# Triangular products of two heads: one PSUM bank per class of product, masked into two tiles

## The chip, the cores and the metric

The kernel runs on one core of one Trainium2 chip. The metric is the device time of one execution in microseconds (us); smaller is better. A core has five engines that run side by side, each through its own list of instructions in a fixed order: TensorE (PE: matmuls out of SBUF into PSUM, with weight loads that the profile lists apart as PEld), VectorE (DVE), ScalarE (ACT), GpSimd (POOL) and SyncE (SP, which here only issues DMAs). They wait for each other through semaphores. PSUM, into which TensorE writes, has eight banks of 512 float32 per partition, on 128 partitions.

## The reference, cut to what matters

The reference is one inference step of two layers, on a prompt of 512 tokens and on eight short sample sequences. Layer 0 is an RWKV-7 time mixing, layer 1 a sparse attention. The change touches only the recurrence of layer 0 for the prompt. There are 16 heads of width 64, and each holds a 64 x 64 state S that every token updates:

```python
def step(S, inp):
    r_t, w_t, k_t, v_t, a_t, b_t = inp
    sa = jnp.einsum('bhij,bhj->bhi', S, a_t)
    S = S * w_t[:, :, None, :] + sa[..., None] * b_t[:, :, None, :] + v_t[..., None] * k_t[:, :, None, :]
    return S, jnp.einsum('bhij,bhj->bhi', S, r_t)
```

The kernel doesn't take the 512 tokens one by one. It takes eight chunks of 64 tokens, and inside a chunk it works with matrices "token by token" (64 x 64). Such a matrix says how much the key of token s adds to the answer of token t. A token sees only earlier ones, so these matrices are triangular: the full product is computed, and a mask (`gmask`) sets the other half to zero.

## The kernel before, in words

`layer0` first projects the inputs, then computes keys, decays and rates (`keys`), inverts small triangular systems (`invert`, `merge`), and then runs the recurrence from about 331 us to 545 us of the profiled span. After that come the output projection of layer 0 (`project_out`, whose matmuls stand under the helper line 326) and layer 1 (`layer1`).

**Heads, pairs and groups.** The 16 heads lie in eight pairs. One head of a pair is on partitions 0 to 63, the other on partitions 64 to 127; `PARS` lists the two halves as `(r, par)`. Four pairs make a group g (0 or 1). The function `chunk(c, g, ...)` handles one chunk c of one group, so it runs 8 x 2 = 16 times. It is a generator. Lines 867 to 911 drive it: the stages that need no state (up to the masks) run for the next chunk while the current chunk goes through the stages that do, group 1 lags two chunks behind group 0, and after each step some "filler" is drawn: the gates, the sample recurrence, the output projection of the first half, all with matmuls of their own.

**One call of `chunk`.**
- Lines 1128 to 1131 load AR (per head the vectors a and r, scaled by the decay, 64 + 64 columns) and BK (per head keys k and b) from DRAM, by SP's queue, into tiles `ab0`/`ab1`.
- For an even chunk, lines 1135 to 1143 transpose the values into `sav`; lines 1146 to 1150 transpose BK into `bt`.
- Lines 1153 to 1159 are the triangular products. There are two classes. **Own** (line 1156): one factor of a head (k for one half of the partitions, b for the other, see line 1025) against both of its columns a and r, 64 x 128 outputs, which land on the head's own partitions. **Other** (line 1159): the other factor against r alone, 64 x 64 outputs, which land on the other half of the partitions. Each class has eight matmuls in a call. Before, there is one bank for each head of the pairs: `pg[0]` takes own and other of the heads with par 0, `pg[1]` those of par 1. The two banks come from the tag `pr`, which has two buffers in all; `pr` also serves the transposes of lines 1135 and 1146 and the output `py` of line 1201, for both groups.
- Lines 1160 to 1165 multiply the products with the mask and write them to two SBUF tiles `G[0]`, `G[1]` of 4 x 128 floats per partition (tag `q0`/`q1`): two instructions of 64 partitions (line 1162, the columns of a) and two of 128 partitions (line 1164, the columns of r), 256 elements per partition each.
- Lines 1169 to 1178 compute `s0` from G's columns of a and from the state; lines 1180 to 1185 apply the inverse; lines 1187 to 1199 make the new state; lines 1201 to 1211 make the output `py` from the state and from G's columns of r.

**What sets the order.** The program text gives priorities only. The whole kernel is built in a `TileContext` with `schedule_with_timeline_sim=True` (line 2119): a planner goes through the instructions with its own model of their times, gives each tile a buffer of its tag when one comes free, and writes down a fixed list for each engine. A matmul whose PSUM tile has no buffer yet is passed over for other work that has. Reads and writes of one PSUM bank by different engines are kept apart bank by bank: a mask of a bank waits for the last matmul into that bank.

Of the kernel before, what the change touches and what calls it, by code (L numbers as in the profile page):

```python
# [13 lines left out]
OP = mybir.AluOpType  # L14
# [207 lines left out]
PARS = [(slice(0, 64), 0), (slice(64, 128), 1)]  # L222


class K:
# [898 lines left out]
    def chunk(self, c, g, NTt, VT, PC, dAR, dBK, STS, Y):  # L1124
        nc = self.nc
        ident, gmask = self.C("ident"), self.C("gmask")
        ps = range(4 * g, 4 * g + 4)
        AR = self.t(f"ab{g}", (128, 4, 2, 64))
        nc.sync.dma_start(AR.rearrange("p i x n -> p i (x n)"), dAR[g][:, :, c])
        BK = self.t(f"ab{g}", (128, 4, 2, 64))  # L1130
        nc.sync.dma_start(BK.rearrange("p i x n -> p (i x) n"), dBK[g][:, :, :, c].rearrange("p i x n -> p (i x) n"))
        if c % 2 == 0:

            tk = c * 64 + (16 if c >= 4 else 0)
            pv = self.t("pr", (128, 4, 2, 64))
            for i, p in enumerate(ps):
                nc.tensor.transpose(pv[:, i].rearrange("p a b -> p (a b)"), VT[p][:, tk:tk + 128], ident)
            for x in range(2):
                r = slice(x * 64, x * 64 + 64)
                sav = self.t(f"q{g}", (128, 4, 2, 64))  # L1140
                for par in range(2):
                    nc.scalar.activation(sav[par * 64:par * 64 + 64, :, par, :], pv[r, :, par, :], AF.Copy)
                self.SA[g, c + x] = sav
        sav = self.SA[g, c]
        yield
        pb = self.t("pr", (128, 4, 128))
        for i in range(4):
            nc.tensor.transpose(pb[:, i], BK[:, i].rearrange("p a b -> p (a b)"), ident)
        bt = self.t(f"q{g}", (128, 4, 128))
        nc.scalar.activation(bt, pb, AF.Copy)  # L1150
        yield

        pg = [self.t("pr", (128, 4, 128)) for _ in range(2)]
        for i in range(4):
            for r, par in PARS:
                nc.tensor.matmul(pg[par][r, i], BK[r, i, par], AR[r, i].rearrange("p a b -> p (a b)"), start=True, stop=True)  # L1156
        for i in range(4):
            for r, par in PARS:
                nc.tensor.matmul(pg[par][PARS[1 - par][0], i, 64:128], BK[r, i, 1 - par], AR[r, i, 1], start=True, stop=True)
        G = [self.t(f"q{g}", (128, 4, 128)) for _ in range(2)]  # L1160
        for r, par in PARS:
            nc.vector.tensor_tensor(G[par][r, :, 0:64], pg[par][r, :, 0:64], gmask[r, None, 0:64].to_broadcast([64, 4, 64]), OP.mult)
        for r, par in PARS:
            nc.vector.tensor_tensor(G[par][:, :, 64:128], pg[par][:, :, 64:128],
                                    gmask[:, None, 64:128].to_broadcast([128, 4, 64]), OP.mult)
        yield
        ST = STS[g]

        s0 = self.t(f"s{g}", (128, 4, 64))
        for i in range(4):  # L1170
            for r, par in PARS:
                nc.tensor.matmul(s0[r, i], G[par][r, i, 0:64], sav[r, i, par], start=(i == 0), stop=(c == 0), skip_group_check=True)
        if c > 0:
            for i in range(4):
                for r, par in PARS:
                    nc.tensor.matmul(s0[r, i], AR[r, i, 0, :], ST[r, i], start=False, stop=True, skip_group_check=True)
        s0s = self.t(f"f{g}", (128, 4, 64))
        nc.vector.tensor_copy(s0s, s0)
        yield
        sa = self.t(f"s{g}", (128, 4, 64))  # L1180
        for i, p in enumerate(ps):
            for r, par in PARS:
                nc.tensor.matmul(sa[PARS[1 - par][0], i], NTt[p][r, c], s0s[r, i], start=True, stop=True)
        nc.vector.tensor_copy(sav[64:128, :, 0, :], sa[64:128])
        nc.vector.tensor_copy(sav[0:64, :, 1, :], sa[0:64])
        yield
        pS = self.t(f"s{g}", (128, 4, 64))
        for i in range(4):
            for r, par in PARS:
                nc.tensor.matmul(pS[r, i], bt[:, i, r], sav[:, i, par], start=True, stop=True)  # L1190
        st = self.t(f"f{g}", (128, 4, 64))
        pc = PC[:, 4 * g:4 * g + 4, c:c + 1].to_broadcast([128, 4, 64])
        if c > 0:
            tt = self.t(f"f{g}", (128, 4, 64))
            nc.vector.tensor_tensor(tt, pS, ST, OP.add)
            nc.vector.tensor_tensor(st, tt, pc, OP.mult)
        else:
            nc.vector.tensor_tensor(st, pS, pc, OP.mult)
        STS[g] = st
        yield  # L1200
        py = self.t("pr", (128, 4, 64))
        if c > 0:
            for i in range(4):
                for r, par in PARS:
                    nc.tensor.matmul(py[r, i], ST[r, i], AR[r, i, 1, :], start=(i == 0), stop=False, skip_group_check=True)
        for i in range(4):
            for r, par in PARS:
                nc.tensor.matmul(py[r, i], sav[:, i, par], G[par][:, i, 64:128], start=(c == 0 and i == 0), stop=True, skip_group_check=True)
        if c % 2 == 0:
            Y[g].append(self.t("p", (128, 2, 4, 64)))  # L1210
        nc.scalar.activation(Y[g][-1][:, c % 2], py, AF.Copy)
        yield
# [910 lines left out]
```

## Time and profile before

| what | value |
|---|---|
| time before, median of 3 runs | 1035.68 us (1035.01 to 1036.47) |
| the profiled execution | 1032.77 us, of which its span is 1031.0 us |
| PE busy (matmuls) | 949.3 us, 92% of the span |
| DVE busy | 666.8 us, 65% |
| ACT busy | 565.8 us, 55% |
| POOL busy | 474.3 us, 46% |
| DMA | 156.69 MB, mean 152 GB/s |

The span is what the profile sees of one execution, from the first to the last instruction; 1.77 us of the execution lie around it. The profiled execution was 2.91 us (0.28%) faster than the median of the other runs. An engine is busy when one of its instructions runs; matmuls overlap each other, so a busy PE says that something was in it, and the time that a set of matmuls takes is read from the start of the first to the start of what follows. A float32 matmul stands in the trace as two records: line 1156 issues 16 x 8 = 128 matmuls and has 256 records. The chain of work follows the last instruction back to what released it, step by step, and so tells which engine was the late one in each stretch.

### The profile page before, as it was taken

What the parts mean: (1) busy time and instruction counts of PE and PEld (TensorE: products, weight loads), DVE (VectorE), ACT (ScalarE), POOL (GpSimd) and SP (SyncE); (2) the same over time, 40 slices, a digit from 0 to 9 for tenths busy, and PEclk for the clock granted to TensorE, in tenths of its full rate; (3) what the DMA queues carried; (4) which work ended last, traced back from release to release, by engine and by line L of the source; (5) the groups of instructions that cost most, each with busy time, mean ns of one, the idle gap of its engine ahead of it and who ended that gap; (6) DMA issues with size and microseconds to landing.
All of it is one profiled execution on the core that took longest, in us unless ns stands there. A gap on an engine that the chain in (4) does not pass through costs nothing.

```text
span 1031.0 us, 24779 instructions
## 1 busy us (share of the span) xinstructions
PE 949.3 (92%) x9429; PEld 845.1 (82%) x9429; DVE 666.8 (65%) x1504; ACT 565.8 (55%) x1333; POOL 474.3 (46%) x573
## 2 busy tenths in 40 slices
PE   5799998989989999999898989999999999987997
PEld 4798997979777868888787988999788887875986
DVE  3797579798486642556966824655785566477554
ACT  4356685556444336435544635656686657475442
POOL 5923558654930363221323475665353547233530
PEclk8798999999999999999998999999999999998999
DMA  5675525648645454655594642332444462454533
GB/s 186 198 258 192 186 68 158 191 132 241 208 134 143 135 169 146 185 149 131 123 274 126 209 142 84 115 109 84 119 125 129 106 164 82 145 166 151 176 122 113
DMA packets 151368, 156.69 MB, mean 152 GB/s; under 512 B 53330, under 2 KB 99954, under 8 KB 150994
## 3 DMA queue, kind: packets, MB, share of 16 engines
q1 hardware_dynamic: 151250, 155.11, 50.6%
q8 instruction: 74, 1.21, 0.5%
q14 instruction: 44, 0.36, 0.1%
HBM read 111.33 MB, written 43.93 MB: 151 GB/s over the span
## 4 chain that ended last, share of the span: by engine, by line
PE 46%; DVE 11%; DMA 6%; POOL 4%; ACT 4%; issue 3%; SPq 1%; DVEq 0%; POOLq 0%; ACTq 0%
PE ph L326 21%; PE pq L1726 3%; PE pw L1820 3%; PE pq L1804 2%; POOL l L288 2%; PE pr L1156 2%; DMA d<-dram 2%; PE ph L2046 1%; ACT a L1760 1%; DVE a L1780 1%; DVE l L288 1%; ACT l L287 1%; PE ph L371 1%; DMA out_swkv<-p 1%; DVE a L1753 1%
## 5 line engine op out<-in xcount | busy, mean ns | idle before, releaser
L326 PE MATMUL ph<-x,l 128*128 128x272 f32 x2448 | 362.6, 299 | 13.4 <-ACT x L287 4.0
L326 PEld LDWEIGHTS ph<-x,l 128*128 128x128 f32 x2448 | 327.7, 193 | 31.5 <-issue 7.3
L288 POOL TENSOR_TENSOR l<-w,l 128x512 fp32r<-128x512 f32 (+2 forms) x118 | 157.7, 1349 | 139.3 <-ACT l L287 120.5
L287 ACT ACTIVATE l<-w 128x512 fp32r<-128x512 f32 (+2 forms) x160 | 93.6, 612 | 100.1 <-PE ph L326 43.6
L326 PE MATMUL pp<-x,l 128*128 128x272 f32 x768 | 111.5, 300 | 6.0 <-POOL l L288 6.0
L326 PEld LDWEIGHTS pp<-x,l 128*128 128x128 f32 x768 | 103.9, 195 | 8.4 <-POOL l L288 6.2
L1760 ACT ACTIVATE a<-a,st 128x512 f32<-128x512 f32 (+3 forms) x128 | 70.7, 554 | 26.5 <-DVE st L1753 25.9
L1753 DVE CUSTOM_DVE_ANT_0 a<-pq,tb 128x512 f32<-128x512 f32 (+3 forms) x128 | 56.7, 484 | 21.3 <-PE pq L1726 21.0
L1726 PE MATMUL pq<-p,z 128*128 128x512 f32 (+7 forms) x288 | 57.0, 326 | 3.1 <-DVE st L1756 1.5
L326 PE MATMUL pp<-t,l 128*128 128x272 f32 x384 | 54.9, 294 | 0.0
L1807 ACT ACTIVATE h<-pq 128x512 f32<-128x512 f32 x60 | 35.4, 591 | 34.0 <-PE pq L1804 27.3
L1804 PE MATMUL pq<-cst,a 128*128 128x128 f32 x320 | 49.5, 278 | 3.7 <-DVE st L1756 1.8
L326 PEld LDWEIGHTS pp<-t,l 128*128 128x128 f32 x384 | 50.8, 190 | 0.9
L1780 DVE TENSOR_SCALAR a<-a,st 128x128 f32<-128x128 f32 (+3 forms) x112 | 50.9, 514 | 0.5
L288 POOL TENSOR_TENSOR d<-d,d 128x544 fp32r<-128x544 f32 (+2 forms) x21 | 28.8, 1370 | 48.4 <-ACT d L287 38.9
L1726 PEld LDWEIGHTS pq<-p,z 128*128 128x128 f32 x288 | 42.3, 189 | 9.7 <-issue 5.0
L288 DVE TENSOR_TENSOR l<-w,l 128x512 fp32r<-128x512 f32 x42 | 35.7, 860 | 15.5 <-ACT l L287 15.3
L1804 PEld LDWEIGHTS pq<-cst,a 128*128 128x128 f32 x320 | 37.0, 141 | 9.9 <-issue 7.6
L1500 DVE TENSOR_TENSOR d<-ph,RS 128x272 f32<-128x272 f32 x56 | 24.1, 436 | 31.1 <-PE ph L326 29.9
L1820 PE MATMUL pw<-h,p 128*64 128x256 f32 x320 | 38.8, 390 | 1.1 <-ACT h L1807 0.7
L1773 POOL TENSOR_TENSOR cc<-cc,st 128x64 f32<-128x64 f32 x32 | 12.6, 395 | 52.7 <-DVE st L1770 43.5
L667 POOL TENSOR_TENSOR d<-d,d 128x544 f32<-128x544 f32 x8 | 11.2, 1397 | 55.7 <-ACT d L385 55.7
(419 smaller groups left out, 2011.1 us busy)
## 6 DMA issues: line engine op xcount, KB each, us to landing
w<-in_rkvz SPq DMA_DIRECT2D x64, 256.0 KB, 2.9
d<-dram SPq DMA_DIRECT2D x54, 272.0 KB, 4.2
w<-in_win SPq DMA_DIRECT2D x56, 256.0 KB, 2.9
dram<-d SPq DMA_DIRECT2D x48, 272.0 KB, 2.6
ab<-dram SPq DMA_DIRECT2D x32, 256.0 KB, 3.6
p<-in_xT SPq DMA_DIRECT2D x16, 272.0 KB, 3.9
tb<-dram SPq DMA_DIRECT2D x16, 264.0 KB, 5.2
dram<-uar SPq DMA_DIRECT2D x8, 512.0 KB, 3.5
```

The source lines that it names most:

```text
L287: nc.scalar.activation(hi, raw, AF.Copy)
L288: (eng or nc.gpsimd).tensor_tensor(lo, raw, hi.bitcast(F32), OP.subtract)
L326: nc.tensor.matmul((pt[h][:m, :HN] if split else pt[:m, h, :HN]), a[:, k, :m], b[:, h * HN:(h + 1) * HN], start=(k == 0 and n == 0), stop= ...
L1156: nc.tensor.matmul(pg[par][r, i], BK[r, i, par], AR[r, i].rearrange("p a b -> p (a b)"), start=True, stop=True)
L1500: self.nc.vector.tensor_tensor(o, p, r, OP.mult)
L1726: nc.tensor.matmul(p[:, par], QZ[k, b][x][:, par, m], kk[:, lo:hi], start=(x == 0), stop=(x == 1))
L1753: nc.vector.tensor_tensor_reduce(out=P[par][j], in0=p[:, par, :n], in1=TB[k][:, g, o:o + n], scale=-1.0, scalar=3.0e38, op0=OP.add, op1=OP ...
L1760: nc.scalar.activation(P[par][j], P[par][j], AF.Exp, scale=-1.0, bias=st[:, 0, g, j + 1:j + 2], accum_out=st[:, 1, g, j + 1:j + 2])
L1780: (nc.gpsimd if e == "p" else nc.vector).tensor_scalar(pj, pj, rr, None, op0=OP.mult)
L1804: nc.tensor.transpose(pt[:, g % 2, g // 2], PB[g][j][:, c * 128:c * 128 + 128], ident)
L1807: nc.scalar.activation(w, pt, AF.Copy)
L1820: nc.tensor.matmul(po[r], v, W[x][:, par], start=False, stop=(x == 0), skip_group_check=True)
```

## The change

The two banks of the products are divided by class and no longer by head. `own` takes the own products of both heads of the pairs (each head on its own partitions, 128 columns per pair); `other` takes the other products of both (64 columns per pair). The masks write two tiles: `GA` for the columns of a of both heads in one instruction of 128 partitions, and `GR` for the columns of r, in four instructions of 64 partitions each. Every mask instruction has 256 elements per partition, as before; there are five where there were four. The readers take the same numbers from the new tiles: `s0` (line 1172) from `GA`, `py` (line 1208) from `GR`. The number and the shapes of the matmuls are the same, and so is the number of tiles taken from `pr` and from `q0`/`q1`.

```diff
-        pg = [self.t("pr", (128, 4, 128)) for _ in range(2)]
+        own, other = self.t("pr", (128, 4, 128)), self.t("pr", (128, 4, 64))
         for i in range(4):
             for r, par in PARS:
-                nc.tensor.matmul(pg[par][r, i], BK[r, i, par], AR[r, i].rearrange("p a b -> p (a b)"), start=True, stop=True)
+                nc.tensor.matmul(own[r, i], BK[r, i, par], AR[r, i].rearrange("p a b -> p (a b)"), start=True, stop=True)
         for i in range(4):
             for r, par in PARS:
-                nc.tensor.matmul(pg[par][PARS[1 - par][0], i, 64:128], BK[r, i, 1 - par], AR[r, i, 1], start=True, stop=True)
-        G = [self.t(f"q{g}", (128, 4, 128)) for _ in range(2)]
+                nc.tensor.matmul(other[PARS[1 - par][0], i], BK[r, i, 1 - par], AR[r, i, 1], start=True, stop=True)
+        GA, GR = self.t(f"q{g}", (128, 4, 64)), self.t(f"q{g}", (128, 2, 4, 64))
+
+        def masked(r, x):
+            return gmask[r, None, x * 64:x * 64 + 64].to_broadcast([r.stop - r.start, 4, 64])
+
+        nc.vector.tensor_tensor(GA, own[:, :, 0:64], masked(slice(0, 128), 0), OP.mult)
         for r, par in PARS:
-            nc.vector.tensor_tensor(G[par][r, :, 0:64], pg[par][r, :, 0:64], gmask[r, None, 0:64].to_broadcast([64, 4, 64]), OP.mult)
+            nc.vector.tensor_tensor(GR[r, par], own[r, :, 64:128], masked(r, 1), OP.mult)
         for r, par in PARS:
-            nc.vector.tensor_tensor(G[par][:, :, 64:128], pg[par][:, :, 64:128],
-                                    gmask[:, None, 64:128].to_broadcast([128, 4, 64]), OP.mult)
+            nc.vector.tensor_tensor(GR[r, 1 - par], other[r], masked(r, 1), OP.mult)
...
-                nc.tensor.matmul(s0[r, i], G[par][r, i, 0:64], sav[r, i, par], start=(i == 0), stop=(c == 0), skip_group_check=True)
+                nc.tensor.matmul(s0[r, i], GA[r, i], sav[r, i, par], start=(i == 0), stop=(c == 0), skip_group_check=True)
...
-                nc.tensor.matmul(py[r, i], sav[:, i, par], G[par][:, i, 64:128], start=(c == 0 and i == 0), stop=True, skip_group_check=True)
+                nc.tensor.matmul(py[r, i], sav[:, i, par], GR[:, par, i], start=(c == 0 and i == 0), stop=True, skip_group_check=True)
```

## The prediction, made before the changed kernel ran

> **What bounds the kernel now.** I read the page first, then busy times by stretch for the recurrence, then the chain of work through it.
>
> ```profile
> span 1031.0 us, 24779 instructions
> PE 949.3 (92%) x9429; PEld 845.1 (82%) x9429; DVE 666.8 (65%) x1504; ACT 565.8 (55%) x1333; POOL 474.3 (46%) x573
> ```
>
> PE is the fullest engine, but that is a mean over stages. The products run only in the recurrence, so I cut that into four stretches (columns: start and end, length, then busy us and instructions of PE, PEld, DVE, ACT, POOL; granted TensorE clock, DMA share, GB/s).
>
> ```profile
> 331.00:395.00 64.00, 60.41 (x836) 48.74 (x836) 33.37 (x65) 24.08 (x49) 27.63 (x27) 0.97 0.50 144
> 395.00:488.00 93.00, 92.81 (x1621) 80.80 (x1622) 47.33 (x112) 45.83 (x107) 26.47 (x22) 1.00 0.54 159
> 488.00:511.00 23.00, 19.51 (x341) 16.17 (x341) 20.43 (x71) 12.76 (x42) 9.33 (x16) 1.00 0.47 111
> 511.00:545.00 34.00, 32.13 (x429) 28.05 (x425) 23.53 (x59) 15.87 (x35) 8.16 (x9) 1.00 0.88 236
> ```
>
> From 395 to 488 PE is busy 92.81 of 93.00 us and DVE only 47.33. From 488 to 511 it turns round: DVE 20.43 of 23.00. From 511 the DMAs are full (0.88). The chain of work (start, us, what) says the same, with the edges between the stretches:
>
> ```profile
> by line: PE pr L1156 13.3%; PE ph L326 11.6%; PE ph L371 8.6%; PE s L1172 5.3%; PE pr L1148 5.0%; PE s L1183 4.8%; PE s L1190 4.6%; PE pr L1208 4.2%; DVE p L733 4.0%; PE s L1176 3.7%; PE pr L1159 3.6%; PE pr L1205 3.3%; PE ph L720 2.7%; DMA
> 386.00 3.48 DMA q<-dram
> 395.18 0.68 PE s L1109 x32
> 491.99 0.43 DVE q L1162
> 508.20 0.79 DVE p L733 x3
> ```
>
> The first row is the share by line of the chain from 395 to 511 us: the own products (L1156) alone are 13.3% of it, more than any other line, and the other products (L1159) 3.6%. Until 386 the chain came through a DMA (and before that through POOL), so PE time saved earlier than 395 moves nothing. From 395.18 it lies on PE; at 491.99 it goes over to DVE.
>
> What follows the recurrence hangs on its end. SP, the DMA queue (waits: total us, times, longest):
>
> ```profile
> SPq L914 <- DVE f L1195: 7.1, 1, 7.1
> 511.74 0.35 SPq L914 DMA_DIRECT2D out_pwkv<-f  x1
> ```
>
> SP stood 7.1 us before line 914, which stores the last state of group 0; the loads behind it make the full DMAs from 511 on. If that state comes earlier, they come earlier. So I take a gain on the chain before 511 to reach the end whole.
>
> **The products on PE, the term that decides.** Timeline and chain rows of PE, four ways in which products and their like run today:
>
> ```profile
> 437.01 0.76 PE L1156 MATMUL pr<-ab,ab 64*64 64x128 f32 x5
> 437.50 0.27 PE L1159 MATMUL pr<-ab,ab 64*64 64x64 f32 x1
> 437.61 0.27 PE L1156 MATMUL pr<-ab,ab 64*64 64x128 f32 x1
> ...
> 438.11 0.39 PE L371 MATMUL ph<-p,p 128*128 128x272 f32 x1
> ...
> 438.88 0.69 PE pr L1156 x5
> 439.97 0.95 PE ph L371 x6
> ...
> 338.99 0.71 PE L1156 MATMUL pr<-ab,ab 64*64 64x128 f32 x10
> 340.06 0.29 PE L1312 MATMUL ph<-p,v 32*32 32x64 f32 x2
> ...
> 461.25 0.65 PE L1156 MATMUL pr<-ab,ab 64*64 64x128 f32 x8
> 461.83 1.02 PE L326 MATMUL ph<-x,l 128*128 128x272 f32 x6
> ...
> 432.89 0.61 PE s L1183 x16
> 433.50 0.70 PE ph L371 x4
> ```
>
> First, a bank alone. Between 437.01 and 438.11 stand eight records of L1156 and eight of L1159, that is four own and four other matmuls (two records each): the products of the heads of one par, one bank. Then PE does something else (L371), and the second bank follows at 438.88, until 439.97. The heads of one par all use the same 64 x 64 part of PE, so the own records start one by one, 0.11 us apart (437.50 to 437.61). A bank costs 1.10 us (438.11 - 437.01), the second 1.09; a call 2.2 us.
>
> Second, both banks at once. At 338.99 the two banks were both free, the planner alternates the two halves, and the records start in pairs: the whole call takes 340.06 - 338.99 = 1.07 us.
>
> Third, 461.25: half of the own products of both heads, alternating (eight records one by one would take 0.9), 0.58 us until L326. The other four matmuls are four more pairs of records, 0.11 us each: a whole own class alone would take 0.58 + 0.44 = 1.02 us.
>
> Fourth, L1183: sixteen records of 64 columns, alternating between the two halves of the partitions, into **one** bank (the tile `s`): 0.61 us. That is the shape of the other class after the change.
>
> After the change a bank holds both halves, so each pass alternates even when the two banks come free at different times: 1.02 + 0.61 = 1.63 us for a call instead of 2.2, a gain of **0.57 us**. If the two passes stand together, it is 1.07, a gain of 1.13 us. A call that had both banks at once already gains nothing. I take 0.57, since the halves stand apart in nearly every call today, and the tag `pr` still has two buffers.
>
> ```profile
> 395.00:488.00 93.00, 18.87 (x147) 14.63 (x148) 1.00 0.54 159
> 488.00:511.00 23.00, 6.33 (x47) 4.69 (x45) 1.00 0.47 111
> ```
>
> These are the L1156 records (PE, then PEld) in two stretches: 147 / 16 = 9 calls between 395 and 488, 47 / 16 = 3 between 488 and 511. Of the nine, the one at 461.25 alternates already. PE term: 8 x 0.57 = **4.6 us**, at most 8 x 1.13 = 9.0, at least 0 (if other work that stands on PE between passes takes the place). The four calls outside 395 to 511 and the three in the DVE stretch I count at nothing on PE: there the chain lies on POOL, DMA and DVE; were PE late there, they would add 7 x 0.57 = 4.0.
>
> The Trainium skill speaks against this. Its page "TensorEngine Tiling (Array Packing)", section "Gotcha 1: PSUM Pressure", says that different row tiles can't access the same PSUM bank at the same time; after the change the two heads of a pair are two row tiles in one bank. The trace disagrees for writes to different partitions: L1183 has just this, and its sixteen records take 0.61 us; one by one, at half of 0.11 us each for 64 columns, they would take some 0.9. What the rule would give is a rival below.
>
> **The masks on DVE.** (Duration ns min/median/max, first and last start.)
>
> ```profile
> L1162 DVE TENSOR_TENSOR q<-pr,cst x32: 406/422/431, 332.8 to 524.9; 64x256 f32<-64x256 f32 x32
> L1164 DVE TENSOR_TENSOR q<-pr,cst x32: 402/415/427, 333.1 to 525.3; 128x256 f32<-128x256 f32 x32
> DVE q L1162 <- PE pr L1159: 22.5, 16, 9.8
> ```
>
> 64 partitions cost as much as 128 (422 and 415 ns), so what counts is the number: five instead of four in each of 16 calls, 16 x 0.42 = 6.7 us more of DVE. Between 395 and 488 it is hidden: DVE is busy 47.33 of 93.00 us, and the 9 x 0.42 = 3.8 us fit. Between 488 and 511 DVE is the chain: 3 x 0.42 = **1.3 us** on the path. The first calls hide behind POOL and DMA, the last behind the full DMAs. If the cover went everywhere, the price would be 6.7.
>
> The masks' waits: today the first mask of a bank waits for the last other product (22.5 us in 16 waits, idle time of an engine that isn't late there). Afterwards GA waits for the own class alone and GR's last two for the other class. No wait is added to the list; behind a waiting mask stand the recurrence's copies (L1178, L1184, L1185) and the state (L1195) of the other group, for which PE waits with L1183 and L1190, as today. `s0` needs GA only and could start sooner; the masks run one chunk ahead of it, so I count nothing. Where the first mask's stall goes, PE is late next, not DVE.
>
> **What costs nothing.** Loads of weights: the same number and shapes. `GR` is read in one run instead of with gaps, `GA` lies alone: no row shows a difference by that, so I take 0, with a few ns each way as bounds. Buffers: two `pr` and two `q` tiles as before; GA is free after `s0` instead of after `py`; a gain or nothing. DMAs: none moves in the text; SP's load of the next BK waits for the last other product, as today.
>
> **Sum.** -4.6 + 1.3 = **-3.3 us**. The profiled execution (1032.77 us, span 1031.0 and 1.77 around it) would become 1029.5. It lies 2.9 below the median of the runs, 1035.68; from that median the forecast is **1032.4 us** (-0.32%).
>
> **Rivals.**
>
> *The passes stand together.* One class ends and the other bank is free at once: -9.0 + 1.3 = -7.7, **1028.0 us**. Against it: only two buffers of `pr`, shared with L1135, L1148 and py; for it: 338.99.
>
> *No change.* The PE gain is taken up again: the DVE stretch holds its 20.43 us of work and begins only when its inputs (finish, gates, loads) are there, or the DMAs from 511 on (share 0.88) don't start earlier. 0 of 4.6 arrives, or no more than the masks take back: **1035.7 us**. For it: three engines are the bound in turn within 150 us.
>
> *The ring of PSUM buffers, the other side.* A bank of `pr` now comes free after three masks (own), the other after two, where it was two and two; 0.42 us more per call before the next transposes (L1148) or `py` (L1205) may start. With two buffers for both groups that decides from the point at which PE runs out of other work while both are held. All 16 calls on the path, 6.7, and the 1.3 of the DVE stretch, less the 4.6: +3.4, **1039.1 us**; with no PE gain +6.7, 1042.4. The planner writes other lists for every engine too, and one bad place is worth as much:
>
> ```profile
> SPq L1131 <- PE pr L1159: 16.9, 5, 6.1
> PEld pr L1205 <- ACT p L1211: 0.9, 2, 0.6
> ```
>
> SP already stood up to 6.1 us at the loads of BK behind the other products. Against the ring: PE waited only 0.9 us for `pr` buffers at L1205, because fillers stand in.
>
> *Row tiles take turns in a bank.* Own records one by one: 1.02 + 8 x 0.11 = 1.90; other, at twice 0.61, 1.2; a call 3.1 instead of 2.2: 8 x 0.9 = 7.2, and 1.3 of masks: +8.5, **1044.2 us**. L1183 speaks against it; only the 128-column form in one bank is unseen. This is the skill's rule named above.
>
> **How the numbers follow.** A measurement of this kernel can tell about 0.2% (2.1 us) from no change: below 1033.6 is faster, above 1037.8 slower. Chances: the forecast 0.45 (its own range 1029 to 1034), together 0.08, no change 0.22, ring or a bad list 0.20, turns 0.05. Of the forecast 0.03 falls within 0.2%. Faster 0.42 + 0.08 = 0.50; same 0.03 + 0.22 = 0.25; slower 0.20 + 0.05 = 0.25. The range goes from the PE bound with a little replanning, 1026, to 1041, between the ring's two prices; outside are the turns and the tails of two rivals.
>
> **What would show it.** Right: own records start in pairs in nearly every call, from own's first record to the next line about 1.0 us, other about 0.6; 80 masks instead of 64, at 0.42 us; PE still full between 395 and 488, that stretch some 4 us shorter; line 914 about 3 us earlier. Wrong: own records one by one; PE idle in that stretch before L1148 or L1205; the chain on DVE before 480; line 914 earlier and the end not.

## The result, and the profile after

The changed kernel takes 1041.3 us in the median (1039.23 to 1045.71, 5 runs); the kernel before took 1035.01 beside it (1029.92 to 1036.47, 5 runs). The ratio is 1.0059, 95% interval 1.003 to 1.0087: slower by 0.6%, where 1032.4 was predicted, and 0.3 us above the top of the range. The ratios and their intervals come from the runs in the chip's usual, fast state, by another estimate than the quotient of the two medians, and can differ from it by up to 0.3%. The profiled execution of the changed kernel took 1043.79 us, with a span of 1042.0; that of before took 1032.77.

From line 1160 on the changed text stands up to four lines lower: the masks are lines 1165 (GA), 1167 (own into GR) and 1169 (other into GR), `py` is 1209 and 1212, its copy 1215.

The products do what the change says. The chain of work of the changed kernel (start, us, what):

```profile
446.98 1.02 PE pr L1156 x16
...
448.82 0.61 PE pr L1159 x16
...
462.55 1.02 PE pr L1156 x16
...
464.86 0.61 PE pr L1159 x16
```

Own takes 1.02 us and other 0.61, the very numbers of the prediction; the first pair holds in spite of what the clock did just before, as shown below. The four stretches of the recurrence, which the prediction shows of before (start and end, length, busy us of PE, PEld, DVE, ACT, POOL, then clock, DMA share, GB/s):

```profile
331.00:395.00 64.00, 60.18 (x832) 48.60 (x832) 34.78 (x67) 24.74 (x50) 28.37 (x27) 0.97 0.48 141
395.00:488.00 93.00, 84.08 (x1527) 72.61 (x1524) 46.28 (x108) 43.28 (x102) 25.43 (x21) 0.94 0.51 149
488.00:511.00 23.00, 18.31 (x356) 14.76 (x354) 19.59 (x61) 10.77 (x30) 6.50 (x9) 0.94 0.52 123
511.00:545.00 34.00, 30.26 (x427) 25.50 (x424) 23.46 (x62) 15.42 (x40) 6.88 (x9) 0.89 0.70 192
```

The second stretch was full before (92.81 of 93.00). Now PE stands for 8.9 us of it, and the granted clock falls to 0.94. So a large part of the loss lies where the gain was expected. (Of the 8.9 us, 3.6 lie before 425 us; they were not followed.) In the third and fourth stretch the clock is lower too, 0.94 and 0.89 where it was 1.00; more on this under "Wait or clock?". Cut finer, around 431 us, the changed kernel shows:

```profile
422.00:431.00 9.00, 7.67 (x218) 7.09 (x219) 7.30 (x18) 1.58 (x3) 1.34 (x1) 1.00 0.79 224
431.60:436.60 5.00, 0.09 (x1) 0.09 (x2) 1.07 (x2) 1.67 (x4) 0.00 (x0) 0.99 0.57 176
436.60:446.80 10.20, 10.20 (x72) 7.94 (x72) 3.97 (x11) 4.35 (x11) 3.16 (x3) 0.50 0.34 104
```

For 5.00 us PE does nothing, and then it works for 10.20 us at a clock of 0.50. In the same 10.20 us of the kernel before, at full clock, twice as much is done:

```profile
436.60:446.80 10.20, 10.20 (x156) 8.95 (x150) 4.69 (x11) 3.34 (x10) 4.08 (x3) 1.00 0.66 203
```

156 matmul records against 72. Who let PE stand? The waits of the changed kernel between 425 and 447 us (engine, what waits, for whom: us, times, longest):

```profile
ACT l L287 <- DMA w<-in_wo: 10.7, 2, 9.8
...
PE pr L1137 <- ACT p L1215: 5.0, 1, 5.0
```

And ScalarE's timeline at this place, first of the changed kernel, then of the kernel before (start, us, line, output<-input, number, idle time ahead):

```profile
423.64 0.60 ACT L1150 ACTIVATE q<-pr 128x512 f32<-128x512 f32 x1 [0.66 <-PE pr L1148]
434.07 0.63 ACT L287 ACTIVATE l<-w 128x512 fp32r<-128x512 f32 x1 [9.83 <-DMA w<-in_wo]
435.56 0.63 ACT L287 ACTIVATE l<-w 128x512 fp32r<-128x512 f32 x1 [0.86 <-DMA w<-in_wo]
436.09 0.64 ACT L1215 ACTIVATE p<-pr 128x256 f32<-128x256 f32 x2
437.65 1.55 ACT L1142 ACTIVATE q<-pr 64x256 f32<-64x256 f32 x4 [0.92 <-PE pr L1137]
```

```profile
427.78 0.38 ACT L1211 ACTIVATE p<-pr 128x256 f32<-128x256 f32 x1 [2.96 <-PE pr L1208]
429.00 0.38 ACT L1211 ACTIVATE p<-pr 128x256 f32<-128x256 f32 x1 [0.84 <-PE pr L1208]
430.65 3.12 ACT L1142 ACTIVATE q<-pr 64x256 f32<-64x256 f32 x8 [1.27 <-PE pr L1137]
434.80 1.29 ACT L287 ACTIVATE l<-w 128x512 fp32r<-128x512 f32 x2 [1.02 <-DMA w<-in_wo]
```

Line 287 is the helper that copies a loaded weight, here the first weight of the output projection (`in_wo`). Before, ScalarE did the two output copies of `py` and the eight copies of `sav` first, and the weight arrived in the meantime (1.02 us of waiting). In the changed kernel's list the two weight copies stand **ahead** of all ten. ScalarE works its list in order, so it stood 9.83 us until the first weight was there (the two loads were issued only at 430.60 and 431.97 us), with two finished `py` tiles behind it; these held both `pr` buffers, and PE, whose next transposes (line 1137) need one, stood until 436.51. No line of this is in the diff. The planner had written other lists for the whole recurrence, on all engines.

### The profile page after: what moved, and what is told of

It is laid out like the page before. It is cut to its first block, busy times and chain, and to the rows that moved or that the text cites. A ratio compares the mean times of both kernels' runs of the same rounds, so it can differ in the third digit from the quotient of the medians.

```text
span 1042.0 us, 24790 instructions
## 1 busy us (share of the span) xinstructions
PE 947.9 (91%) x9429; PEld 842.1 (81%) x9429; DVE 671.3 (64%) x1520; ACT 565.9 (54%) x1333; POOL 473.2 (45%) x573
## 4 chain that ended last, share of the span: by engine, by line
PE 45%; DVE 11%; ACT 5%; DMA 5%; POOL 4%; issue 4%; SPq 1%; DVEq 0%; POOLq 0%; ACTq 0%
PE ph L326 21%; PE pq L1730 3%; PE pw L1824 3%; PE pq L1808 2%; DMA w<-in_wo 2%; POOL l L288 2%; ACT a L1764 1%; PE pr L1156 1%; DVE a L1784 1%; DVE l L288 1%; PE ph L2050 1%; ACT l L287 1%; PE ph L371 1%; PE s L1194 1%; DMA d<-dram 1%
```

## The experiments

**Theory A**: the other lists are the loss, and the products' gain is real. **Theory B**: the change itself costs, by the fifth mask and the shared ring of PSUM buffers. **Theory C**: the denser products draw the clock down. Later two more came up about the size of the loss: D (half of it is the halved clock) and E (it is the wait alone). In the experiments' kernels a few lines are added, so their line numbers stand up to seven higher.

**The fault put into the kernel before.** Its two `py` copies are queued behind the two weight copies, nothing else is told to the planner:

```diff
+                if h == 0 and m == 0:
+                    for e in (self.ev[2, 0], self.ev[0, 1]):
+                        for u in self.cut[-2:]:
+                            self.tc.add_manual_dep(e.ins, u.ins.name, mybir.DependencyInfo(
+                                mybir.DependencyClass.NoSync, mybir.DependencyReason.DATA), reason="order")
...
```

> The kernel before, with the two py copies on ScalarE queued behind the two copies of the first output weight, as they stand in the changed kernel; products and masks as before. Theory A: PE idles some 5 us near 431 and the clock halves after it: 1040 to 1046. Rivals B and C: no change, 1034 to 1037.

Measured: 1043.6 us against 1035.07, ratio 1.0075 (1.0051 to 1.01). Its profile has the wait and the half clock (ScalarE's timeline, then the stretch at half clock; PE's gap ahead of its work is 3.5 us here):

```profile
437.30 1.27 ACT L289 ACTIVATE l<-w 128x512 fp32r<-128x512 f32 x2 [10.16 <-DMA w<-in_wo]
```

```profile
436.60:443.40 6.80, 4.51 (x21) 4.51 (x22) 3.71 (x7) 3.99 (x10) 3.29 (x3) 0.50 0.40 110
```

Without any of the change, the run with this order lost as much as the change did. It isn't the price of the two copies alone: the planner answered with other lists for TensorE, VectorE and the DMA queue from about 430 us on, which the trace shows.

**The fault taken out of the changed kernel, in two steps.** First the two `py` copies alone are put ahead of the weight copies:

```diff
+                with ExitStack() as behind:
+                    if h == 0 and m == 0:
+                        for e in (self.ev[2, 0], self.ev[0, 1]):
+                            behind.enter_context(self.tc.issue_after(e.ins))
...
```

> The changed kernel with one thing put back: in ScalarE's list the two copies of the first output weight (line 287, out of the w<-in_wo loads) stand again behind the two copies of py (line 1215) that they stand ahead of since the change. In the changed kernel PE idled 5.0 us there and the granted clock was halved for 10.2 us right after. Theory A (the planner's order on ScalarE is the loss; the products' gain is real): about 5 us of idle PE and about 5 us of halved clock go, so 1031 to 1034 us, at or below the kernel before, and no half clock near 437 us. Rival B (ring of PSUM buffers and the fifth mask): no change, 1039 to 1042. Rival C (denser matmuls draw the clock down by themselves): the halved clock stays, 1036 to 1040.

Measured: 1039.11, ratio 1.0043 (1.0021 to 1.0065), where theory A had 1031 to 1034 and no half clock. Part of the loss is left (between 431 and 440 us the clock is still 0.62), and ScalarE's timeline shows what else stands in the way:

```profile
426.79 0.85 ACT L1220 ACTIVATE p<-pr 128x256 f32<-128x256 f32 x2 [6.24 <-PE pr L1217]
429.88 0.63 ACT L288 ACTIVATE l<-w 128x512 fp32r<-128x512 f32 x1 [2.23 <-DMA w<-in_wo]
431.99 0.63 ACT L288 ACTIVATE l<-w 128x512 fp32r<-128x512 f32 x1 [1.48 <-DMA w<-in_wo]
432.52 3.10 ACT L1147 ACTIVATE q<-pr 64x256 f32<-64x256 f32 x8
```

The eight `sav` copies (here line 1147) still stand behind the weight. So they are put ahead too:

```diff
-                        for e in (self.ev[2, 0], self.ev[0, 1]):
-                            behind.enter_context(self.tc.issue_after(e.ins))
+                        for e in ((2, 0), (0, 1), ("sav", 4, 0), ("sav", 2, 1)):
+                            behind.enter_context(self.tc.issue_after(self.ev[e].ins))
...
```

Against the changed kernel five instructions move, and all others keep their order: two weight copies on ScalarE, the two subtractions of VectorE that follow them, and one load on the DMA queue. (Each leaves one position and takes another, which makes the ten of the expectation below.)

> The changed kernel with the first output weight's copies behind the two output copies and behind the eight copies of the next chunk's values, where the kernel before has them; ten instructions moved, all else stands in the changed lists. Theory A, the loss in two places: the wait near 430 and the halved clock at 436 are gone, the second place (490 to 525) stands: 1034 to 1038, faster than the run with only the output copies moved (1039.1). If the second place was only a consequence of the first: 1031 to 1034. Theories B and C: 1040 to 1044.

Measured: 1033.41 against 1037.16 of the kernel before in the same session, ratio 0.9974 (0.9946 to 1.0001). ScalarE now does the ten copies while the weight comes, and PE is full behind them at full clock (ScalarE's timeline, then the stretch):

```profile
427.56 0.85 ACT L1220 ACTIVATE p<-pr 128x256 f32<-128x256 f32 x2 [6.24 <-PE pr L1217]
429.21 3.12 ACT L1147 ACTIVATE q<-pr 64x256 f32<-64x256 f32 x8 [0.81 <-PE pr L1142]
432.36 1.24 ACT L288 ACTIVATE l<-w 128x512 fp32r<-128x512 f32 x2
```

```profile
429.00:439.20 10.20, 10.20 (x134) 8.42 (x134) 6.08 (x15) 7.21 (x18) 2.85 (x4) 1.00 0.65 201
```

From 1.0059 to 0.9974, in two sessions, is 0.85%, some 9 us, for five instructions. The time is the one expected if the second place (490 to 525) were only a consequence of the first, but the trace doesn't bear that out: between 488 and 511 us its clock is 0.85, where it was 0.94 in the changed kernel.

**The change in the lists of before.** To measure the edits without the planner, the lists themselves were held. The two programs differ, engine by engine, only in the sixteen additional masks and in which product is which, so each instruction has its counterpart. A table with the order of the kernel before is added, and each instruction of an engine is queued behind its forerunner:

```diff
+def pin(nc, tc):
+    ins = {i.name: i for i in nc.cur_bb.bb.instructions}
+    for line in zlib.decompress(base64.b85decode(ORDER)).decode().splitlines():
...
+        for a, b in zip(names, names[1:]):
+            tc.add_manual_dep(ins[b], a, mybir.DependencyInfo(mybir.DependencyClass.NoSync, mybir.DependencyReason.DATA))
...
         build(nc, tc, ctx, I, O)
+        pin(nc, tc)
```

> The changed kernel's instructions, each put where the kernel before has its counterpart, on all five engines (the sixteen products of a call into the places of its sixteen, own pass first; the fifth mask right after the fourth). Nothing is left out. Theory A (the planner's other lists are the loss; the products' gain is real): the loss near 430 is gone, no halved clock at 436 us, and the gain of the products is left over: about 1032, faster than before by 2 to 5 us (1030 to 1034). Theory B (the fifth mask and the shared ring of PSUM buffers are the loss): as slow as the changed kernel, 1039 to 1043. Theory C (the denser products bring the halved clock themselves): halved clock between 400 and 525 us as in the changed kernel, 1038 or more.

Measured: 1032.89 against 1037.16, ratio 0.9941 (0.992 to 0.9963). In a second session:

> The changed kernel in the lists of the kernel before, once more and beside the changed kernel: 1031 to 1034 by theory A, some 9 us below the changed kernel; 1036 or more if its first result was luck of the chip.

Measured: 1031.25 against 1035.2, ratio 0.9946 (0.9915 to 0.9976). In the lists of before, the change **gains** 4.3 and 4.0 us by the medians (by the ratios some 6 us, with bounds from 2.5 to 8.8). By its medians it is the fastest version of the study. B and C both fall: the masks, the ring and the denser products are all in it, and the clock stays at 0.99 to 1.00 in the rows below. The recurrence as a whole, before and with the change in the lists of before (shifted, since this execution came to the recurrence 5.6 us later and left it 4.4 later), and then the stretch that was full before:

```profile
331.00:545.00 214.00, 204.86 (x3218) 173.75 (x3219) 124.67 (x306) 98.54 (x231) 71.59 (x73) 0.99 0.57 161
```

```profile
336.60:549.40 212.80, 197.83 (x3219) 165.52 (x3220) 131.53 (x322) 98.88 (x231) 71.88 (x73) 0.99 0.58 162
399.00:492.00 93.00, 89.97 (x1638) 76.72 (x1634) 51.75 (x123) 46.79 (x109) 26.46 (x22) 1.00 0.56 160
```

PE is busy 7.0 us less (204.86 to 197.83), with the same matmuls; DVE 6.9 us more, for sixteen more instructions. But the stretch is only 1.2 us shorter (214.00 to 212.80): in this execution 5.8 of the 7.0 us became idle time of PE, 2.8 of them where PE was full before (third row: 3.0 us idle, 0.2 before). That lists made for the slower products hold the order may be the reason; it was not tested. So the size of the gain stays open between these rows and the medians; one execution decides little (runs of this kernel lie between 1023.19 and 1041.6).

**The fifth mask alone**, first with lists as the planner writes them, then in the lists of before. One of the four masks is split into two halves of 64 partitions:

```diff
-            nc.vector.tensor_tensor(G[par][:, :, 64:128], pg[par][:, :, 64:128],
-                                    gmask[:, None, 64:128].to_broadcast([128, 4, 64]), OP.mult)
+            for q in ([slice(0, 128)], [slice(0, 64), slice(64, 128)])[par]:
+                nc.vector.tensor_tensor(G[par][q, :, 64:128], pg[par][q, :, 64:128],
+                                        gmask[q, None, 64:128].to_broadcast([q.stop - q.start, 4, 64]), OP.mult)
```

> The kernel before, with one of its four masks split into two halves of 64 partitions: five masks, products by head as before. Theory A: within 1.5 us of before (1034 to 1037), since DVE has room but for the stretch from 488 to 511. Rival B: 16 x 0.42 = 6.7 us of DVE on the path, 1039 to 1043.

> The kernel before with one mask split in two halves, so that each call has five, all lists pinned to those of before. Theory A: sixteen more masks hide beside TensorE except for the last calls, so at most 1.3 us: 1034.5 to 1037, less than or equal to the run with the fifth mask under planned lists (1037.6). Theory B: 16 masks by 0.42 us on the path, up to 6.7 us: 1038 to 1042.

Measured: 1037.63 against 1035.07 with the planner's lists, ratio 1.0025 (1.0002 to 1.0049); 1037.14 against 1037.16 in the lists of before, 0.9992 (0.997 to 1.0015). With lists held, the mask costs nothing that the runs can tell from zero. The first figure, 0.6 us above what theory A allowed, may be a price of other lists (the planner did write others here); the two intervals overlap, so this is not shown. In the stretch that PE fills, it hides as forecast: with the lists of before, DVE goes from 47.33 to 50.41 us and PE stays full:

```profile
395.00:488.00 93.00, 92.91 (x1621) 80.89 (x1622) 50.41 (x121) 45.72 (x107) 26.47 (x22) 1.00 0.54 159
```

The masks are the same in number here and in the change in the lists of before. What is left between the two, 1037.14 - 1032.89 = 4.3 us by the medians, is the products and their tiles.

**The kernel before in the changed lists.** The same table the other way round, for all engines but PE, whose list is the planner's:

> The kernel before, with its four masks and its two banks of one parity each, its ScalarE, VectorE, GpSimd and DMA lists put in the order of the changed kernel; TensorE's list is the planner's. Theory A: the loss comes without the change, with the wait for w<-in_wo of about 10 us ahead of the output copies and the halved clock behind it: 1042 to 1047, for the products' gain is missing. Theory B and C: 1034 to 1037, as before.

Measured: 1053.38, ratio 1.013 (1.0104 to 1.0156). The direction is A's, the size more than any theory gave. ScalarE's timeline has the same wait, so it comes with the lists and without the change:

```profile
436.04 0.63 ACT L289 ACTIVATE l<-w 128x512 fp32r<-128x512 f32 x1 [9.58 <-DMA w<-in_wo]
```

The loss is 16.2 us by the medians, some 8 us more than the change ever cost. What those are was not followed; PE's list in this run is a third one, neither that of before nor that of the changed kernel.

**Wait or clock?** In the changed kernel with its own lists (held by a table as above), the one call of sixteen records ahead of the gap (line 1187, into `sa`) is made eight times, with the same result each time, so that PE is busy while it would stand. ScalarE's wait is left as it is:

```diff
-        for i, p in enumerate(ps):
-            for r, par in PARS:
-                nc.tensor.matmul(sa[PARS[1 - par][0], i], NTt[p][r, c], s0s[r, i], start=True, stop=True)
+        for _ in range(8 if (c, g) == (3, 0) else 1):
+            for i, p in enumerate(ps):
+                for r, par in PARS:
+                    nc.tensor.matmul(sa[PARS[1 - par][0], i], NTt[p][r, c], s0s[r, i], start=True, stop=True)
...
```

> The changed kernel in its own lists, and in the one call ahead of the wait near 431 us the sixteen records of the state products into sa (0.68 us a pass) are made eight times in place of once, so that TensorE is busy some 4.3 of the 5.0 us in which it stood; ScalarE's wait for w<-in_wo and all lists stay. Theory D (half of the loss is the halved clock that follows the idle stretch): no halved clock at 436 us, so about 5 us less than the changed kernel, half of the 10.2 us for which it ran at half: 1036 to 1039 where the changed kernel has 1041 to 1044. Theory E (the loss is the wait itself, what comes behind it would have waited for something else anyway): as the changed kernel, within 1.5 us.

Beside it ran the changed kernel, once more:

> The changed kernel once more, for the comparison on the same chip: 1041 to 1044 by every theory, with the halved clock at about 436 us.

Measured: 1038.59 with PE kept busy, ratio 1.0031 (1.0005 to 1.0056); 1041.77 without, 1.0058 (1.0033 to 1.0083). The 10.2 us behind the gap, first with PE kept busy, then without:

```profile
436.83 0.66 PE L1139 MATMUL pr<-cst,p 128*128 128x128 f32 x4 [1.59 <-ACT p L1218]
```

```profile
436.80:447.00 10.20, 10.17 (x124) 8.33 (x125) 6.51 (x16) 5.92 (x16) 4.52 (x4) 1.00 0.31 98
```

```profile
436.15 1.11 PE L1137 MATMUL pr<-cst,p 128*128 128x128 f32 x4 [5.36 <-ACT p L1215]
```

```profile
436.10:446.30 10.20, 10.15 (x74) 7.89 (x74) 4.03 (x10) 4.56 (x12) 3.16 (x3) 0.53 0.33 102
```

After a gap of 1.59 us the clock stays at 1.00 and 124 records are done; after 5.36 us it is 0.53, and 74. The medians lie 3.2 us apart where D gave about 5 and E less than 1.5. The direction is D's; the two intervals overlap, so the 3.2 us are a rough size. The two profiled executions took the same in all (1043.68 and 1043.70 us), yet the place itself can be priced in them. From the two output copies behind the wait to the next output copy, ScalarE's timeline has (first with PE kept busy, then without):

```profile
436.42 0.64 ACT L1218 ACTIVATE p<-pr 128x256 f32<-128x256 f32 x2
451.58 0.39 ACT L1218 ACTIVATE p<-pr 128x256 f32<-128x256 f32 x1 [1.31 <-PE pr L1215]
```

```profile
435.73 0.64 ACT L1215 ACTIVATE p<-pr 128x256 f32<-128x256 f32 x2
454.98 0.38 ACT L1215 ACTIVATE p<-pr 128x256 f32<-128x256 f32 x1 [1.31 <-PE pr L1212]
```

That is 15.16 us against 19.25, with the same work in the same lists: in these two profiles the half clock cost 4.1 us, which is near D's price and not E's.

The clock falls a second time in most of these profiles. In the changed kernel:

```profile
508.00:511.00 3.00, 3.00 (x60) 2.77 (x56) 2.94 (x11) 0.50 (x2) 0.24 (x1) 0.54 0.02 4
518.00:525.00 7.00, 6.40 (x61) 5.64 (x60) 5.56 (x15) 1.83 (x5) 1.09 (x2) 0.53 0.20 51
```

With the weight copies put back and with PE kept busy, the clock between 488 and 511 us is 0.85; with the fifth mask alone in the lists of before it is 0.93. So this second place hangs neither on the first nor on the denser products alone. What it costs was not tested.

An earlier run of the changed kernel, beside the first three experiments:

> The changed kernel once more, on the same chip as the others. All theories: 1039 to 1044. Theory A: again some 5 us of idle PE near 432 and the halved clock after it, since both follow from the fixed list. Rival C: the halved clock also where PE didn't idle.

Measured: 1043.64, ratio 1.0091 (1.0049 to 1.0133). With the first result and the one above, the changed kernel lay 0.6% to 0.9% above the kernel before in three sessions.

**The recurrence alone.** Runs of one kernel lie up to 18 us apart. The recurrence scatters less: from the start of the first product to the issue of the last store of the state (line 914 and its counterparts), three profiles of the changed kernel agree within 0.7 us. Each other row is one profile, the row of the change in the lists of before two:

| kernel | recurrence in us |
|---|---|
| before | 212.9 |
| changed | 221.5, 221.1, 221.7 |
| changed, output copies first | 217.2 |
| changed, weight copies last | 211.4 |
| changed, in the lists of before | 211.6, 211.0 |
| before with the fifth mask, planner's lists | 213.6 |
| before with the fifth mask, in the lists of before | 214.7 |
| changed, PE kept busy | 215.0 |
| before with late copies | 225.1 |
| before, in the changed lists | 229.8 |

The changed kernel in the planner's lists is 8 to 9 us longer than before, and the five instructions bring 10 us back. The change in the lists of before is 1.2 and 1.9 us shorter than before, and 3.1 and 3.7 us shorter than before with five masks.

## Why the prediction was wrong, step by step

- **What bounds the kernel: right.** PE from 395 to 488, DVE from there to 511. The loss could be so large because PE had no slack in that stretch: PE's 5.00 us of standing had to come out later.
- **The products: right in mechanism and nearly in size.** Predicted were 1.02 + 0.61 us a call where a call took 2.2, and -4.6 us in all, between 0 and -9.0. The rows show 1.02 and 0.61; with lists held, the change as a whole, forecast at -3.3 us, gained 4.3 and 4.0 us by the medians and 1.2 and 1.9 us in the recurrence of the two profiles. PE's busy time fell by 7.0 us over the recurrence, of which 5.8 became idle time in the profile shown.
- **Row tiles in one bank: the rival at 1044.2 falls.** The rule of the Trainium skill, page "TensorEngine Tiling (Array Packing)", section "Gotcha 1: PSUM Pressure", is not borne out here: own's sixteen records of both row halves take 1.02 us in one bank, where one by one they would have taken 1.90 by the prediction's estimate.
- **The masks: right.** Predicted 6.7 us more of DVE, measured 6.9; predicted hidden but for 1.3 us, measured -0.8 us with an interval of -3.1 to +1.6 (0.9992, 0.997 to 1.0015, of 1037.16), and 1.8 us in the recurrence of one profile.
- **The sum: the step that failed.** "DMAs: none moves in the text" is true of the text only. The sum added up the edits as if each list stood still around them. In a kernel whose lists a planner writes from a model of all durations, an edit that is made sixteen times gives the planner another problem, and it moved work that the edit never touches. In the sum that term stood at nothing: the one bad place cost some 9 us (from 1.0059 to 0.9974), about twice the gain, and line 914, forecast some 3 us earlier, came 9.0 us later (520.78 against 511.74).
- **The rival that named it was priced by the wrong thing.** "The planner writes other lists for every engine too, and one bad place is worth as much" stood under the ring of PSUM buffers and took over its price, +3.4 us. The ring and the fifth mask showed no such cost. That 1041.3 lies between this rival's two prices, 1039.1 and 1042.4, is luck; and PE stood before line 1137, a third user of `pr`, not before L1148 or L1205, where the prediction looked for it. A price for the place could have been read beforehand: PE full, two `pr` buffers for products, transposes and `py`, ScalarE as the only engine that empties `py`, and in ScalarE's list weight copies that wait for transfers. If one such copy moves ahead of the `py` copies, PE can stand until the transfer has landed. "PE waited only 0.9 us for `pr` buffers" held for the old lists alone.
- **The clock was missing.** No step counted what an idle stretch of PE does to the clock behind it: 4.1 us in the place above.

Open: why the planner put the weight copies first was not tried. Whether anything of the changed lists besides this place costs time is not settled either: with the five instructions put back the ratio is 0.9974 (0.9946 to 1.0001), with all lists held 0.9941 (0.992 to 0.9963), and the intervals overlap. The second place of the half clock, 500 to 525 us, was not followed.

## What to carry to other kernels

Where a planner writes the lists, measure an edit twice: as planned, and with the old lists held; the first says what you ship, the second tells more of what the edit itself is worth. In a prediction, price the replanning from the profile: find the instruction that waits for a transfer on the engine that empties PSUM, and ask what PE does if it moves ahead of an emptying copy. When such a place is found, a few lines that fix the order there (here five instructions) can take the loss away.

## What the runs showed of the hardware

A gap of some 5 us in PE's work cost more than its length. Behind gaps of 5.00 and 5.36 us the granted clock was 0.50 for 10.20 us and 0.53 in such a stretch, though PE was busy all the time; behind 1.59 us, in the same lists, it stayed at 1.00. At half speed 10.20 us of work lose 5.1 us by this reckoning; 4.1 us were measured between the same two output copies. The length of a gap alone doesn't decide: in the second place of the changed kernel the clock was 0.54 from 508 to 511 us and 0.53 from 518 to 525, and the longest gaps in the ten us ahead of these stretches were 2.37 us (ended at 507.28) and 1.28 us (ended at 516.35). The Trainium skill, page "TensorE: Matmul & The Clock Gate", section "Part 1: The HAM clock gate", has the half rate after an idle window of about 3.4 us; the rows behind the gaps of 5.00 and 5.36 us agree, those of the second place are not explained by it. It has the full rate back after at least one busy window of about 3.4 us; here it took three times as long (10.20 us with PE busy 10.20), and less in the kernel before with late copies, whose row of 6.80 us at 0.50 has PE busy for 4.51.
